# One adaLN gate and one layer's SSM preparation moved from VectorE to GpSimd

## The chip, the cores and the metric

The kernel runs on one NeuronCore of a Trainium2 chip. The metric is the device time of one execution in microseconds (us), the median of several runs. The engines are named as the profile names them: PE (TensorE matmul) and PEld (its weight load), DVE (VectorE), ACT (ScalarE), POOL (GpSimd) and SP (SyncE, which issues nearly all DMAs here). PEq, SPq and so on are the engines' instruction queues.

## The reference

Two layers of a hybrid decoder, sequence 256, model width 1024, all in float32:

```python
for l in range(2):
    mod = silu(c) @ w_ada[l] + b_ada[l]
    sh1, sc1, g1, sh2, sc2, g2 = split(mod, 6)            # 1024 each
    h = rmsnorm(x, norm1_g[l]) * (1 + sc1) + sh1
    u, dq, dk, dv, mq, mk, mv = split(h @ w_in[l])
    mix = concat(s5_mixer(u, ...), diff_attention(...), moba_attention(...))
    x = x + g1 * (mix @ w_out[l])
    h = rmsnorm(x, norm2_g[l]) * (1 + sc2) + sh2
    x = x + g2 * (relu(h @ mlp_w1[l])**2 @ mlp_w2[l])
return rmsnorm(x, final_g)
```

The S5 mixer is a complex diagonal state-space model. Before it can run in a layer it needs small weights made from the parameters (complex products of C and B with constants of the discretisation) and tables of sines and cosines for 128 steps of 8 pairs of groups.

## The kernel before

**Big products.** The weights come from HBM in units of 128 x 1024 floats (512 KB). `raw_unit` (L104) issues the DMA of a unit on SP into a ring `raw` of 3 buffers. `unit` (L112) splits it into a high part (ACT, L123) and a low part (DVE, L124) in a ring `whl` of 4 buffers, because each float32 product is made of three fp32r matmuls on PE (`mm3`, L129). A `raw` buffer comes free when both have read it, a `whl` buffer when PE has used it. The down projection of the MLP (`mlp2`, L983) uses two matmuls per tile of the hidden layer (L991, L992).

**adaLN vectors.** `mod` is 6 vectors of 1024 per layer, each a product of `silu(c)` with 8 units of `w_ada`. Those that are needed first are made by `ada_first`. The others go through `ada_two` (L283): it loads two units into the ring `ada` of 3 buffers and does one of two things. For most vectors PE multiplies them (`ada_mm`, L255). For the five in `ADA_DVE`, (layer 0, vector 2) and (layer 1, vectors 0 to 3), DVE accumulates them into one tile `adaacc`, scaled by a column of `cs` (L296, L298), and after the 8th unit four small matmuls sum over the partitions (L303). Vector (0, 2) is the gate g1 of the first mixer. Its units are asked for by the steps `D1` of the first layer's list of steps `MIXER[0]` (four pairs), those of layer 1 by the slots of the first layer's MLP (`ada_step_dve`, L1142). Steps `P` in the list ask for the units that PE multiplies, from the same ring `ada`. The gate is used in `back_add` after the output projection.

**SSM preparation.** `ssm_weights` (L595) gives three steps: two complex products of 128 x 256 tiles, with sign changes, for `cv`, and one for `ab` (22 elementwise instructions of 128 x 256 in all, lines 616 to 631). `ssm_tables` (L562) gives four steps `turns` (ACT instructions on L575 to L577, then three on engine `e`, L578 to L580) and one `sines` (ACT, and on `e` L588, twice). For layer 1 both are prepared in the first layer's MLP, one step per two slots from j = 1 on (L1143 to L1149), under `tc.issue_after` of the last DVE and ACT instruction. That call orders only instructions of the same engine as the one it names.

**Order.** Each engine runs its queue in order. SP's queue holds the DMAs of `raw`, `ada` and some others, and one whose buffer isn't free holds all those behind it. The order within the queues is not that of the text: a planner with costs of its own moves instructions, so that steps of the list interleave.

**POOL** builds a few constants at the start and adds up squares in the second half of each MLP (`square_in`, L1003, lines 1008 and 1010).

Of the kernel before, what the change touches and what calls it, by code (L numbers as in the profile page):

```python
# [14 lines left out]
OP = mybir.AluOpType  # L15
# [7 lines left out]
MAGIC = 12582912.0  # L23
# [31 lines left out]
def hybrid_trunk(ctx, tc, xT_d, pos_d, par_d, lqk_d, sb_d, sbt_d, scw_d, glu_d, wm_d, wa_d, out_d):  # L55
# [7 lines left out]
    V, A, T, GP = nc.vector, nc.scalar, nc.tensor, nc.gpsimd  # L63
# [4 lines left out]
    def wk_tile():  # L68
        return psum.tile([128, 512], F32, name="wk")
# [145 lines left out]
    cs = const.tile([128, 8], F32)  # L215
# [9 lines left out]
    def ada_finish(l, i, row):  # L225

        rs = work.tile([128, 256], F32, name="adarow", bufs=1)
        A.activation(rs, row, AF.Copy)

        def end():  # L230
            cp = wk_tile()
            for b in range(2):
                T.matmul(cp[:, 4 * b:4 * b + 4], rs[:, b * 128:(b + 1) * 128], ident[:, 0:128:32], start=True, stop=True)
            V.tensor_tensor(mod[l][:, i * 8:i * 8 + 8].rearrange("p (g b) -> p b g", b=2),
                            cp[:, 0:8].rearrange("p (b g) -> p b g", b=2),
                            col("b_ada", l * 48 + i * 8, 8).rearrange("p (g b) -> p b g", b=2), op=OP.add)
        return end
# [45 lines left out]
    def ada_two(l, i, k):  # L283

        ws = []
        for kk in (k, k + 1):
            w = ring.tile([128, UW], F32, name="ada", bufs=3)
            nc.sync.dma_start(w, wa_d[16 + ADA.index((l, i)) * 8 + kk])
            ws.append(w)
        if (l, i) in ADA_DVE:  # L290
            if k == 0:
                ada_st[l, i] = big.tile([128, UW], F32, name="adaacc", bufs=1)
            acc = ada_st[l, i]
            for j, w in enumerate(ws):
                if k + j == 0:
                    V.tensor_scalar(acc, w, cs[:, 0:1], None, op0=OP.mult)  # L296
                else:
                    V.scalar_tensor_tensor(acc, w, cs[:, k + j:k + j + 1], acc, op0=OP.mult, op1=OP.add)  # L298
            if k == 6:
                def fin():  # L300
                    row = wk_tile()[:, :256]
                    for g in range(4):
                        T.matmul(row[32 * g:32 * g + 32, :], ones, acc[:, g * 256:(g + 1) * 256], start=True, stop=True,  # L303
                                 tile_position=(0, 32 * g), skip_group_check=True)
                    return ada_finish(l, i, row)
                ada_fin_dve.append(fin)
        else:
            if k == 0:
                ada_st[l, i] = wk_tile()[:, :256]
            row = ada_st[l, i]  # L310
            for j in range(2):
                ada_mm(row, k + j, ws[j:j + 1])
            if k == 6:
                ada_fin.append(lambda: ada_finish(l, i, row))
# [247 lines left out]
    def ssm_tables(l, e):  # L562

        ct = big.tile([128, 8, 128], F32, name="tb_c")
        st = big.tile([128, 8, 128], F32, name="tb_s")
        TABS[l] = (ct, st)
        sh = [128, 2, 128]

        def turns(p):
            k = work.tile(sh, F32, name="sg_z")  # L570
            c = l * 8 + p
            a, r = ct[:, p:p + 2], st[:, p:p + 2]
            for j in range(2):
                i = slice(c + j, c + j + 1)
                A.activation(a[:, j], tau, AF.Copy, scale=f1[:, i])  # L575
                A.activation(r[:, j], tau, AF.Copy, scale=f2[:, i])
                A.activation(k[:, j], tau, AF.Identity, scale=f12[:, i], bias=magic)  # L577
            e.scalar_tensor_tensor(k, k, MAGIC, a, op0=OP.subtract, op1=OP.subtract)  # L578
            e.tensor_tensor(r, r, k, op=OP.subtract)
            e.tensor_scalar(r, r, -0.4999999, 0.4999999, op0=OP.max, op1=OP.min)  # L580

        def sines():
            for hp in range(0, NP, 4):
                r, c = st[:, hp:hp + 4], ct[:, hp:hp + 4]
                A.activation(c, r, AF.Sin, scale=math.pi)
                A.activation(r, r, AF.Sin, scale=2.0 * math.pi)
                A.activation(c, c, AF.Square)
                e.tensor_scalar(c, c, -2.0, 1.0, op0=OP.mult, op1=OP.add)  # L588
        return [lambda p=p: turns(p) for p in range(0, NP, 2)] + [sines]
# [340 lines left out]
    for l in range(L):  # L930
        V.tensor_scalar(subg[:, l:l + 1], col("subln", l), math.sqrt(128.0) * (1.0 - (0.8 - 0.6 * math.exp(-0.3 * l))), None,
                        op0=OP.mult)
# [66 lines left out]
    def x_rest():  # L999

        return (7,), sqsum[0], ones[:, 0:1], [work.tile([128, S], F32, name="sq", bufs=3)]
# [70 lines left out]
    for l in range(L):  # L1072
        mixed = [big.tile([128, 2, S], F32R, name=f"mx{k}") for k in range(KT)]

        if l == 0:
            h = hs
            cu, cm, cv_ = chunks
            uT = cu.u_out()
            v_m = cv_.values()
        else:  # L1080
            h = norm_h(l, "n1", 0, 1, x_rest(), vec)
            uT = Chunk("u", h).run().u_out()
            cm = Chunk("qk", h).run(1)
            v_m = None
        g2 = work.tile([128, 2, S], F32, name="g2", bufs=1)
        at, qk, accs = {}, {"m": cm}, []
        mix = {"m": slice(6, 8), "0": slice(2, 4), "1": slice(4, 6), "s": slice(0, 2)}
        for t in MIXER[l].split():
            o, a = t[0], t[1:]
            if o == "P":  # L1090
                ada_step(int(a), (l, 4))
            elif o == "D":
                ada_step_dve(int(a))
            elif o == "C":
                qk[a] = Chunk("qk", h).run()
            elif o == "R":
                at[a] = Attn(l, rope_T(qk[a]), v_m if a == "m" else None, a != "m", mixed[mix[a]])
            elif o == "S":
                ssm_two(l, int(a), uT)
            elif o == "E":  # L1100
                at[a[0]].scores(int(a[1]))
            elif o == "V":
                at[a].v = Chunk("v", h).run().values()
            elif o == "W":
                at[a[0]].values(int(a[1]))
            elif o == "F":
                at[a].finish()
            elif o == "Y":
                y = wk_tile()[:, :S]
                ssm_y(l, int(a), uT, y.rearrange("p (s b) -> p s b", s=2))  # L1110
                ssm_gelu(l, int(a), y, uT, g2)
            elif o == "O":
                ssm_out(l, g2, mixed[0:2])
            elif o == "K":
                if not accs:
                    accs = [acc_tile() for _ in range(4)]
                back_unit(accs, mixed[mix[a]], a == "m", False)
        while ada_fin or ada_fin_dve:
            flush(ada_fin)
            flush(ada_fin_dve)  # L1120
        vec = ada_load(l, 5)
        back_unit(accs, mixed[4:6], False, True)
        back_add(accs, l, 2)
        h = norm_h(l, "n2", 3, 4, x_ssq(), vec)
        slot = 0
        for half in range(2):
            acts = []
            for i in range(16):
                if i < 8:
                    acts += mlp1_act(mlp1_mm(h, 0 if half else i + 1), 2 * i)  # L1130
                else:
                    if half and l + 1 < L and i == 15:
                        vec = ada_load(1, 4)
                    mlp2(l, i - 8, acts)
                    if half and i < 15:
                        square_in(i - 8)
                j, odd = divmod(slot, 2)
                slot += 1
                if not odd:
                    continue  # L1140
                ada_step(1, (l, 5))
                ada_step_dve((0, 1, 1, 1, 2, 1, 2, 1, 2, 1, 1, 1, 1, 1, 0, 0)[j] if l == 0 else 0)  # L1142
                if l + 1 < L and j >= 1:  # L1143
                    if j == 1:
                        todo = list(ssm_weights(l + 1, V)) + ssm_tables(l + 1, V)
                        loads[l + 1]()
                    if todo:
                        with tc.issue_after(last_dve[0].ins), tc.issue_after(last_act[0].ins):
                            todo.pop(0)()  # L1149
                    elif j == 12:  # L1150
                        with tc.issue_after(last_mm[0].ins):
                            ssm_weights_pe(l + 1)
                        with tc.issue_after(last_act[0].ins):
                            rsqrt_table()
# [124 lines left out]
```

## Time and profile before

| | |
|---|---|
| median of 3 runs | 690.89 us (690.33 to 696.8) |
| the profiled execution | 694.18 us, span 692.5 us |
| PE busy in the span | 662.6 us (96%) |
| DVE busy | 508.6 us (73%) |
| ACT busy | 385.4 us (56%) |
| POOL busy | 19.2 us (3%), 23 instructions |
| granted TensorE clock | 0.997 of full |

Busy time is the time in which an engine works on an instruction. A row of the timeline gives start, duration, engine, line, operation, output and inputs, and in brackets how long the engine was idle before it and what ended that. Matmuls are pipelined, so the duration of one is longer than the distance to the next.

### The profile page before, as it was taken

To read this page: it belongs to the slowest core of one execution; us is meant where nothing else is said; L and a number is where in the kernel's file an instruction comes from. 1 tells how busy PE (TensorE), PEld (TensorE's weight loads), DVE (VectorE), ACT (ScalarE), POOL (GpSimd) and SP (SyncE) were. 2 spreads that over 40 slices of the span, in tenths; PEclk is the share of its full clock that TensorE was granted. 3 is DMA by queue.
4 is the path that set the end of the run, shared out by engine and by line. 5 is a ranking of instruction groups with operands and counts; after the bars stand their busy time and mean duration, and the time that the engine had idled before them with its cause. 6 is when DMAs were issued, how large, how long until landed. Compare 5 with 4: busy or idle time off the path is not lost. (4 is left out here: it accounts for less than half of the span.)

```text
span 692.5 us, 13248 instructions
## 1 busy us (share of the span) xinstructions
PE 662.6 (96%) x5134; PEld 576.0 (83%) x5134; DVE 508.6 (73%) x1148; ACT 385.4 (56%) x730; POOL 19.2 (3%) x23
## 2 busy tenths in 40 slices
PE   4998999999999999999999999999999999999994
PEld 1785777988899888998887878799899988999883
DVE  5869879976997887868657799876875655555653
ACT  4557555664566833677443547576476633566540
POOL 0000000000000000000220000000000000000220
PEclk9999999999999999999999999999999999999998
DMA  8986786863889698879855632554356555555531
GB/s 299 405 314 210 256 301 219 297 224 117 310 300 320 217 336 257 292 282 327 308 183 182 213 123 64 166 183 147 113 163 203 183 183 183 183 183 183 188 117 61
DMA packets 45278, 152.22 MB, mean 220 GB/s; under 512 B 5152, under 2 KB 5280, under 8 KB 45216
## 3 DMA queue, kind: packets, MB, share of 16 engines
q1 hardware_dynamic: 44640, 150.60, 63.1%
q10 hardware_dynamic: 576, 0.79, 0.4%
q8 instruction: 40, 0.66, 0.4%
q14 instruction: 22, 0.18, 0.1%
HBM read 150.32 MB, written 1.05 MB: 219 GB/s over the span
## 5 line engine op out<-in xcount | busy, mean ns | idle before, releaser
L124 DVE TENSOR_TENSOR whl<-raw,whl 128x1024 fp32r<-128x1024 f32 x178 | 217.4, 1224 | 109.5 <-ACT whl L123 106.7
L123 ACT ACTIVATE whl<-raw 128x1024 fp32r<-128x1024 f32 x178 | 187.8, 1056 | 149.9 <-DMA raw<-in_wm_dram 51.0
L132 PE MATMUL wk<-hx,whl 128*128 128x256 f32 x1536 | 188.5, 284 | 2.2 <-DVE hx L440 1.2
L132 PEld LDWEIGHTS wk<-hx,whl 128*128 128x128 f32 x1536 | 185.4, 192 | 5.5 <-DVE hx L440 2.5
L991 PE MATMUL acc<-mx,whl 128*128 128x512 f32 x256 | 92.1, 399 | 0.0
L992 PE MATMUL acc<-mx,whl 128*128 128x256 f32 x256 | 71.9, 281 | 0.0
L991 PEld LDWEIGHTS acc<-mx,whl 128*128 128x128 f32 x256 | 48.1, 188 | 12.1 <-issue 0.8
L298 DVE SCALAR_TENSOR_TENSOR adaacc<-ada,cs,adaacc 128x1024 f32<-128x1024 f32 x35 | 44.8, 1280 | 9.2 <-DMA ada<-in_wa_dram 9.1
L132 PE MATMUL acc<-mx,whl 128*128 128x256 f32 x384 | 51.1, 288 | 0.0
L132 PEld LDWEIGHTS acc<-mx,whl 128*128 128x128 f32 x384 | 47.4, 191 | 2.8 <-issue 2.7
L992 PEld LDWEIGHTS acc<-mx,whl 128*128 128x128 f32 x256 | 48.4, 189 | 0.3 <-DVE whl L124 0.3
L991 PE MATMUL acc<-at_e,whl 128*128 128x512 f32 x128 | 46.6, 398 | 0.0
L994 DVE SCALAR_TENSOR_TENSOR xall<-acc,mod,xall 128x256 f32<-128x256 f32 x64 | 30.9, 482 | 21.0 <-PE acc L992 20.2
L132 PE MATMUL acc<-whl,hx 128*128 128x256 f32 x288 | 40.0, 288 | 0.0
L132 PEld LDWEIGHTS acc<-whl,hx 128*128 128x128 f32 x288 | 36.5, 191 | 3.1 <-issue 2.2
L784 PE MATMUL acc<-whl,hx 128*128 128x512 f32 x96 | 38.7, 403 | 0.0
L783 PE MATMUL acc<-whl,hx 128*128 128x512 f32 x96 | 38.2, 401 | 0.0
L785 PE MATMUL acc<-whl,hx 128*128 128x512 f32 x96 | 38.0, 396 | 0.0
L992 PE MATMUL acc<-at_e,whl 128*128 128x256 f32 x128 | 35.9, 280 | 0.0
L972 ACT ACTIVATE sp_pa<-wk 128x512 f32<-128x512 f32 x32 | 18.9, 590 | 28.0 <-PE wk L132 28.0
L991 PEld LDWEIGHTS acc<-at_e,whl 128*128 128x128 f32 x128 | 24.0, 188 | 5.9
L439 ACT ACTIVATE hx<-hz,mod 128x256 fp32r<-128x256 f32 x32 | 14.9, 502 | 21.1 <-DVE hz L434 21.1
(352 smaller groups left out, 986.9 us busy)
## 6 DMA issues: line engine op xcount, KB each, us to landing
raw<-in_wm_dram SPq DMA_DIRECT2D x184, 512.0 KB, 4.0
ada<-in_wa_dram SPq DMA_DIRECT2D x74, 512.0 KB, 5.6
sp_gc<-in_wa_dram SPq DMA_DIRECT2D x9, 256.0 KB, 5.1
qT<-in_wa_dram SPq DMA_DIRECT2D x4, 512.0 KB, 8.7
adaacc<-in_wa_dram SPq DMA_DIRECT2D x3, 512.0 KB, 7.8
qk<-in_wa_dram SPq DMA_DIRECT2D x6, 256.0 KB, 5.4
vv<-in_wa_dram SPq DMA_DIRECT2D x6, 256.0 KB, 3.8
at_o<-in_wa_dram SPq DMA_DIRECT2D x6, 256.0 KB, 4.5
```

Of the source, the lines that this page charges most:

```text
L123: A.activation(hi, w, AF.Copy)
L124: V.tensor_tensor(lo, w, hi.bitcast(F32), op=OP.subtract)
L132: last_mm[0] = T.matmul(out, a[:, p, :], b[:, q, :], start=start and i == 0, stop=stop and i == 2, skip_group_check=True)
L298: V.scalar_tensor_tensor(acc, w, cs[:, k + j:k + j + 1], acc, op0=OP.mult, op1=OP.add)
L439: last_act[0] = A.activation(hi, z, AF.Identity, bias=mvec(l, i_sh, k))
L783: T.matmul(o, h[:, 0, sl], w[:, 0, :], start=(k == 0), stop=False, skip_group_check=True)
L784: T.matmul(o, h[:, 0, sl], w[:, 1, :], start=False, stop=False, skip_group_check=True)
L785: last_mm[0] = T.matmul(o, h[:, 1, sl], w[:, 0, :], start=False, stop=last, skip_group_check=True)
L972: A.activation(r, ps, AF.Relu)
L991: T.matmul(acc, w[:, 0, sl], a.rearrange("p c t -> p (c t)"), start=(k == 0), stop=False, skip_group_check=True)
L992: last_mm[0] = T.matmul(acc[:, :S], w[:, 1, sl], a[:, 0, :], start=False, stop=(k == 15), skip_group_check=True)
L994: V.scalar_tensor_tensor(xT[f], acc[:, c * S:(c + 1) * S], mvec(l, 5, f), xT[f], op0=OP.mult, op1=OP.add)
```

## The change

The accumulation of the units of layer 0's vector in `ada_two` is done on GpSimd, in two instructions per unit in place of one: it scales the unit in its `ada` buffer, and adds it to the accumulator. `ssm_weights` and `ssm_tables` of layer 1 get GpSimd as their engine. One instruction of `turns` stays on VectorE.

```diff
             for j, w in enumerate(ws):
-                if k + j == 0:
+                if l == 0:
+                    GP.tensor_scalar(acc if k + j == 0 else w, w, cs[:, k + j:k + j + 1], None, op0=OP.mult)
+                    if k + j:
+                        GP.tensor_tensor(acc, acc, w, op=OP.add)
+                elif k + j == 0:
                     V.tensor_scalar(acc, w, cs[:, 0:1], None, op0=OP.mult)
                 else:
                     V.scalar_tensor_tensor(acc, w, cs[:, k + j:k + j + 1], acc, op0=OP.mult, op1=OP.add)
...
-            e.scalar_tensor_tensor(k, k, MAGIC, a, op0=OP.subtract, op1=OP.subtract)
+            V.scalar_tensor_tensor(k, k, MAGIC, a, op0=OP.subtract, op1=OP.subtract)
             e.tensor_tensor(r, r, k, op=OP.subtract)
             e.tensor_scalar(r, r, -0.4999999, 0.4999999, op0=OP.max, op1=OP.min)
...
-                        todo = list(ssm_weights(l + 1, V)) + ssm_tables(l + 1, V)
+                        todo = list(ssm_weights(l + 1, GP)) + ssm_tables(l + 1, GP)
```

## Rows read from the trace of the kernel before

**Rows 1.** The page, busy time of each engine: us, share of the span, instructions.
```profile
PE 662.6 (96%) x5134; PEld 576.0 (83%) x5134; DVE 508.6 (73%) x1148; ACT 385.4 (56%) x730; POOL 19.2 (3%) x23
```

**Rows 2.** Stretches: length, busy PE, PEld, DVE, ACT, POOL, clock, DMA share, GB/s.
```profile
62.00:131.00 69.00, 66.48 (x530) 50.06 (x527) 61.27 (x185) 38.58 (x98) 0.00 (x0) 1.00 0.76 275
...
175.00:270.00 95.00, 93.57 (x651) 85.72 (x652) 81.51 (x127) 56.08 (x95) 0.00 (x0) 1.00 0.84 293
```

**Rows 3.** Waits of PE from 62 to 131 us: total us, times, longest.
```profile
PE wk L255 <- DMA ada<-in_wa_dram: 2.1, 3, 1.4
PE wk L821 <- ACT qT L822: 0.4, 1, 0.4
```

**Rows 4.** Tile adaacc from 55 to 170 us: count, ns min/median/max, first and last start.
```profile
L303 PE MATMUL wk<-adaacc,ones x8: 379/391/403, 155.2 to 156.7; 128*32 128x256 f32 x8
L298 DVE SCALAR_TENSOR_TENSOR adaacc<-ada,cs,adaacc x7: 1274/1281/1289, 71.1 to 128.1; 128x1024 f32<-128x1024 f32 x7
L296 DVE TENSOR_SCALAR adaacc<-ada,cs x1: 724/724/724, 67.9 to 67.9; 128x1024 f32<-128x1024 f32 x1
```

**Rows 5.** Timeline of POOL, both halves' accumulation of squares: start, duration.
```profile
331.82 1.19 POOL L1008 TENSOR_SCALAR sqs<-sq 128x256 f32<-128x256 f32 x1 [329.81 <-ACT sq L1005]
...
341.74 1.36 POOL L1010 TENSOR_TENSOR sqs<-sqs,sq 128x256 f32<-128x256 f32 x1 [5.08 <-ACT sq L1005]
...
661.45 1.30 POOL L1010 TENSOR_TENSOR sqs<-sqs,sq 128x256 f32<-128x256 f32 x1 [4.34 <-ACT sq L1005]
...
678.40 0.73 POOL L1010 TENSOR_TENSOR sqs<-sqs,sq 128x256 f32<-128x256 f32 x1 [4.36 <-ACT sq L1005]
```

**Rows 6.** Timeline of DVE beside the first two of these.
```profile
331.03 1.28 DVE L298 SCALAR_TENSOR_TENSOR adaacc<-ada,cs,adaacc 128x1024 f32<-128x1024 f32 x1
332.22 1.42 DVE L124 TENSOR_TENSOR whl<-raw,whl 128x1024 fp32r<-128x1024 f32 x1
...
341.28 1.23 DVE L124 TENSOR_TENSOR whl<-raw,whl 128x1024 fp32r<-128x1024 f32 x1
```

**Rows 7.** DVE groups by shape, whole span: count, busy us, mean ns.
```profile
L682 DVE TENSOR_TENSOR sp_pa<-sp_pa,sp_pb 128x256 f32<-128x256 f32 x8 | 3.4, 420 | 0.0
...
L580 DVE TENSOR_SCALAR tb_s<-tb_s 128x256 f32<-128x256 f32 x8 | 2.3, 286 | 0.0
```

**Rows 8.** Timeline of DVE: the second unit's accumulation, and a later split.
```profile
71.15 1.29 DVE L298 SCALAR_TENSOR_TENSOR adaacc<-ada,cs,adaacc 128x1024 f32<-128x1024 f32 x1 [1.91 <-DMA ada<-in_wa_dram]
...
78.83 1.20 DVE L124 TENSOR_TENSOR whl<-raw,whl 128x1024 fp32r<-128x1024 f32 x1
```

**Rows 9.** Timeline of SP's queue from 72 us.
```profile
72.46 0.33 SPq L288 DMA_DIRECT2D ada<-in_wa_dram  x1
72.83 0.43 SPq L109 DMA_DIRECT2D raw<-in_wm_dram  x1
```

**Rows 10.** Tile raw from 72 to 73 us: the one DMA, issue to landing.
```profile
DMA to landing us min/median/max: 5.3/5.3/5.3
```

**Rows 11.** Timeline of ACT: the split of the unit that this DMA brings.
```profile
78.27 1.06 ACT L123 ACTIVATE whl<-raw 128x1024 fp32r<-128x1024 f32 x1 [1.67 <-DMA raw<-in_wm_dram]
```

**Rows 12.** Timeline of PE's weight loads: the first use of that unit.
```profile
80.08 0.19 PEld L784 LDWEIGHTS acc<-whl,hx 128*128 128x128 f32 x1 [0.33 <-DVE whl L124]
```

**Rows 13.** Timeline of SP's queue, the raw DMA behind the second pair.
```profile
92.89 0.38 SPq L109 DMA_DIRECT2D raw<-in_wm_dram  x1
```

**Rows 14.** Timeline of ACT from 98 us.
```profile
98.69 1.04 ACT L123 ACTIVATE whl<-raw 128x1024 fp32r<-128x1024 f32 x1
```

**Rows 15.** Timeline of SP's queue: the last load for layer 1's SSM weights.
```profile
174.76 0.42 SPq L600 DMA_DIRECT2D sp_gc<-in_scw_dram  x1
```

**Rows 16.** Timeline of DVE: a split, and the first instruction of the SSM weights.
```profile
195.85 1.22 DVE L124 TENSOR_TENSOR whl<-raw,whl 128x1024 fp32r<-128x1024 f32 x1 [1.39 <-ACT whl L123]
...
204.38 0.42 DVE L616 TENSOR_TENSOR cv<-sp_gc,kre 128x256 f32<-128x256 f32 x1
```

**Rows 17.** Timeline of PE: the last eight units of the first up projection.
```profile
200.99 23.28 PE L132 MATMUL wk<-hx,whl 128*128 128x256 f32 x192
```

## The prediction

> **What bounds the kernel now.** I read the page first: PE is busy 96% of the span [rows 1], and POOL, which takes the moved work, is nearly empty. The reader is to see that PE can win at most what it idles, and where. The table of stretches gives that: from 62 to 131 us, where the gate's units are accumulated, PE is busy 66.5 of 69.0 us, and from 175 to 270 us, where layer 1's SSM weights and most of its tables are made, 93.6 of 95.0 us [rows 2]. So 2.5 and 1.4 us lie open in the places the change touches. DVE is full in both: 61.3 of 69.0 (89%) and 81.5 of 95.0 (86%). The waits of PE say whether that hurts: in the first stretch PE waits for DMAs of units that it multiplies itself and once for ACT, never for DVE [rows 3]. DVE is busy but ahead of PE, by little. Last I read the timelines for how little: which unit arrives just in time.
>
> **Prices on POOL.** An add of two 128x256 tiles takes 0.73 us when nothing is in its way; the others take about 1.3 us [rows 5]. The row at 341.74 ends at 343.10, and L124 on DVE, 341.28 to 342.51 [rows 6], ends 0.59 us before it: POOL waits for the split to end. Widths of 1024 are not in the trace on POOL. Bounds: no growth (0.7 us), and growth by four (2.9 us). DVE grows by 2.9 for an add (0.42 [rows 7] to 1.23 us [rows 6]) and by 2.5 for a scaling (0.29 [rows 7] to 0.72 us [rows 4]). With these factors the add costs 0.73 x 2.9 = 2.1 us. A scaling of width 256 ends 0.70 us after the L298 in its way (333.01 against 332.31 [rows 5, 6]), so one of 1024 costs 0.70 x 2.5 = 1.8 us. A unit thus takes 3.9 us on POOL where it took 1.28 us on DVE.
>
> **Removed.** DVE loses 7 x 1.28 + 0.72 = 9.7 us in the first stretch [rows 4]. In the MLP it loses 22 weight instructions (18 x 0.42 + 4 x 0.29 us) and ten of the tables (4 x 0.42, 4 x 0.29, and two of width 512 that I put at 0.42 us): 12.4 us. What PE can get back is bounded by its idle time, 2.5 + 1.4 us, and by 0, since it doesn't wait for DVE there; I take 0.
>
> **Added, the ring of loads.** A unit's `ada` buffer is free only when POOL has added it. The second unit lands at 71.15, where DVE stopped waiting for it, and DVE was through at 72.44 [rows 8]. At 72.46 SP issues the `ada` load that had waited for that buffer, and at 72.83, behind it in the queue, the DMA of a `raw` unit [rows 9], which lands 5.3 us later [rows 10]. ACT has stood idle 1.67 us for it [rows 11], L124 splits it from 78.83 to 80.03 [rows 8], and the weight load at 80.08 has waited 0.33 us for just this split [rows 12]. There is no slack in this chain. On POOL the unit is free at 71.15 + 3.9 = 75.05, 2.6 us later, and PE comes 2.6 us later to that product. Ends: 0.1 us (0.7 + 0.7 us on POOL) and 4.4 us (5.7 us on POOL). **I take 2.6.**
>
> The second pair holds the `raw` DMA at 92.89 [rows 13] in the same way. It could have landed at 98.2, ACT took it at 98.69 without a wait for the DMA [rows 14]; 2.6 us later makes it 2.1 us late for ACT. PE doesn't wait for a split here [rows 3], so I take 0 of 0 to 2.1. The last two pairs need 4 x 3.9 = 15.6 us on POOL. Even if it began only at 128.1, with DVE's last addition, it would end at 143.7, and the matmuls that sum over the partitions come at 155.2 [rows 4]: the gate itself costs nothing. Without those 11.5 us of cover PE would stand still at L303 with the output projection behind it.
>
> **Added, DVE against POOL.** One row shows DVE held by POOL: L124 at 332.22 took 1.42 instead of 1.23 us [rows 6] while POOL's scaling, waiting since 331.82, got its turn [rows 5]. So a POOL scaling of 256 costs the DVE instruction behind it 0.2 us. For an add, with twice the input, I use 0.4 us; its bounds are 0 and the 0.59 us. In the first stretch 15 POOL instructions at 0.2 x 2.5 = 0.5 us, or 1.0 for adds, make 8 x 0.5 + 7 x 1.0 = 11 us of delay against 9.7 us taken off DVE, which also idles 69.0 - 61.3 = 7.7 us: 0.
>
> In the MLP the POOL instructions are not held by the ordering calls, which bind DVE and ACT only. The last load they need is issued at 174.76 [rows 15], and by the 5.3 us of [rows 10] it has landed at about 180, while on DVE the work began at 204.38 [rows 16]. So it moves into the stretch in front, which is the fullest. The split of 195.85 to 197.07 [rows 16] is, by count, the unit in front of the eight that PE begins at 200.99 (192 matmuls in 23.28 us, 0.121 us each [rows 17]); PE needs it at about 200.99 - 24 x 0.121 - 0.4 (four small matmuls) = 197.7. It has 0.6 us of slack, and DVE idled 1.39 us in front of it: 2.0 us of cover. From 180 to 195.85 POOL gets in some ten instructions, one for each of DVE's of 1.2 us. At 0.2 us each that is 2.0, covered; at 0.4 us 4.0, so 2.0 late; at 0.59 us 3.9 late. **I take 1.0**, between the first two.
>
> The tables add a way from DVE over POOL to ACT: the last two `turns` write a buffer that POOL must have read, 0.3 to 0.9 us later each than now, and the splits of ACT queue behind. I cost it at 0 under the four `whl` buffers; without that cover it is up to 1.8 us.
>
> **The sum.** The profiled execution took 694.18 us; + 2.6 + 1.0 gives 697.8. It stands 3.3 us above the median of the runs, 690.89, so the median becomes 694.5 us.
>
> **A rule against the change.** By the row at 332.22 DVE lost 0.2 us to a POOL instruction of 0.7 us [rows 5, 6]. The Trainium skill, "SBUF — State Buffer", section "Who interferes with whom", says that the two share a port pair with an exclusive lock: a VectorE instruction with two SBUF inputs and a GpSimd one that reads SBUF block each other fully, for the whole instruction. POOL's waits agree, DVE's 0.2 us doesn't, and by that rule the time would be that of the next case.
>
> **Rival: DVE is held for POOL's whole instructions, and becomes the bound.** 8 x 1.8 + 7 x 2.1 = 29.1 us of POOL in the first stretch, against 17.4 us that DVE then has free: 0 to 11.7 us too much, as its instructions that read PSUM are hit or spared; I take 5. In the MLP 3.9. With the 2.6 us of the ring: 690.89 + 11.5 = 702.4 us, from 698 to 711. It decides once an add of 1024 holds DVE for more than about 1.5 us. Against it stands the one row.
>
> **Rival: nothing comes late.** The planner may put the `raw` DMA in front of the `ada` load, or start the pairs earlier, since it orders by costs and POOL's differ; or POOL's instructions hardly grow with width. Then the change does its work unseen: 688.4 (2.5 us of idle time returned) to 691.5 us. For it: queues are visibly not in the order of the text. Against it: the chain at 72 to 80 us is tight by 0.0 us.
>
> **Rival: DVE's relief counts.** All 3.9 us of idle time return: 687.0 us. More would need another order of PE's own work, which the profile doesn't offer.
>
> **Chances.** A measurement of this kernel can tell about 1%, 6.9 us, from no change. Forecast (691.5 to 697.8) 0.52, nothing late 0.25, the lock 0.20, relief 0.03. Slower than 697.8: all but 0.01 of the lock and 0.03 of the forecast's upper end, 0.22. Faster than 684.0: 0.03, with a new order of the queues. The same: 0.75. The range of 688 to 702 us leaves out the upper half of the lock and most of the relief.
>
> **What would show it.** A later `raw` DMA than 72.83 and a longer wait of PE for L124 near 80 us show the ring; POOL rows of 1.8 and 2.1 us the prices; L124 or L298 longer than 1.3 us, or gaps beside POOL rows, the lock; the first L616 on POOL near 181 us and a wait for L124 near 198 us the MLP's term. I am wrong if PE waits in none of these places, or if the gate's last sum on POOL comes after 155 us and PE stops at L303.

## The result and the profile after

The changed kernel takes **712.8 us** (median of 6 runs, 709.82 to 717.87) against 690.69 us of the kernel before beside it: 1.0325 times as long, 95% interval 1.029 to 1.0359. The forecast was 694.5 us, the range 688 to 702 us. It was wrong, and beyond the rival that would have made it slower too (702.4 us).

The profiled execution took 710.61 us, its span is 709.0 us. On its page, busy time by engine [rows 1 for before]:

```profile
PE 665.9 (94%) x5134; PEld 578.6 (82%) x5134; DVE 517.0 (73%) x1108; ACT 385.1 (54%) x730; POOL 100.6 (14%) x70
```

The work moved (POOL 19.2 to 100.6 us), yet DVE is busy 8.4 us longer with 40 instructions fewer. The stretches [rows 2], with one between them that I had not looked at:

```profile
62.00:131.00 69.00, 60.96 (x447) 43.68 (x447) 58.54 (x167) 31.75 (x86) 29.25 (x11) 0.93 0.65 227
131.00:175.00 44.00, 37.86 (x334) 35.03 (x334) 30.92 (x71) 23.74 (x58) 12.99 (x5) 0.96 0.58 196
175.00:270.00 95.00, 89.98 (x699) 80.95 (x698) 78.92 (x100) 55.39 (x101) 37.45 (x30) 1.00 0.74 255
```

PE gets through 447 matmuls in the first stretch where it got through 530, and the clock is no longer 1.00. By the first matmul of the up projection PE is 14.9 us late (189.70 against 174.82 us). The profiled executions lie 16.4 us apart, so nearly all of it is lost in the first mixer. POOL there, the first pair and the last five units [rows 5 is all that before showed of POOL]:

```profile
64.43 3.34 POOL L296 TENSOR_SCALAR adaacc<-ada,cs 128x1024 f32<-128x1024 f32 x1 [62.41 <-DVE whl L124]
67.76 3.00 POOL L296 TENSOR_SCALAR ada<-ada,cs 128x1024 f32<-128x1024 f32 x1
70.84 2.38 POOL L298 TENSOR_TENSOR adaacc<-adaacc,ada 128x1024 f32<-128x1024 f32 x1
...
124.14 2.35 POOL L298 TENSOR_TENSOR adaacc<-adaacc,ada 128x1024 f32<-128x1024 f32 x1
126.47 3.28 POOL L296 TENSOR_SCALAR ada<-ada,cs 128x1024 f32<-128x1024 f32 x1
129.84 2.39 POOL L298 TENSOR_TENSOR adaacc<-adaacc,ada 128x1024 f32<-128x1024 f32 x1
132.19 2.86 POOL L296 TENSOR_SCALAR ada<-ada,cs 128x1024 f32<-128x1024 f32 x1
135.13 2.49 POOL L298 TENSOR_TENSOR adaacc<-adaacc,ada 128x1024 f32<-128x1024 f32 x1
137.60 4.08 POOL L296 TENSOR_SCALAR ada<-ada,cs 128x1024 f32<-128x1024 f32 x1
141.75 2.41 POOL L298 TENSOR_TENSOR adaacc<-adaacc,ada 128x1024 f32<-128x1024 f32 x1
```

A unit behind the first takes POOL 5.3 to 6.6 us, not 3.9. Now SP's queue from 121 us. Each DMA goes out as soon as an addition above has ended (126.49, 132.23, 137.62, 144.16 us):

```profile
121.17 0.38 SPq L109 DMA_DIRECT2D raw<-in_wm_dram  x1
126.52 0.33 SPq L288 DMA_DIRECT2D ada<-in_wa_dram  x1
132.25 5.73 SPq L264 DMA_DIRECT2D ada<-in_wa_dram  x2
138.03 0.42 SPq L273 DMA_DIRECT2D qk<-in_wa_dram  x1
144.19 0.33 SPq L264 DMA_DIRECT2D ada<-in_wa_dram  x1
144.62 0.37 SPq L273 DMA_DIRECT2D qk<-in_wa_dram  x1
145.08 0.86 SPq L109 DMA_DIRECT2D raw<-in_wm_dram  x2
```

For 24 us no `raw` DMA is issued. L264 loads the next vector into the same ring `ada`. The `raw` DMAs behind it are the weights of the output projection. What follows is read in the timelines of ACT, DVE and PE:

```profile
150.73 1.06 ACT L123 ACTIVATE whl<-raw 128x1024 fp32r<-128x1024 f32 x1 [6.48 <-DMA raw<-in_wm_dram]
```
```profile
151.82 1.22 DVE L124 TENSOR_TENSOR whl<-raw,whl 128x1024 fp32r<-128x1024 f32 x1 [4.18 <-ACT whl L123]
152.97 0.16 DVE L147 SCALAR_TENSOR_TENSOR at_rq<-rs_t,rs_i 128x4 f32<-128x4 f32 x1
153.16 0.76 DVE L920 TENSOR_TENSOR at_on<-at_o,at_rq 128x256 f32<-128x256 f32 x2
```
```profile
153.73 0.68 PE L925 MATMUL wk<-ident,at_on 128*128 128x128 f32 x4 [1.92 <-DVE at_on L920]
```

ACT waits 6.48 us for the unit, DVE 4.18 us for ACT. The last step of a chain of small instructions (L147), which does not need the unit, stands behind that split in DVE's queue, and PE waits 1.92 us for what L920 makes of its result.

A second effect is on DVE's timeline. Three rows begin while an addition is at work (the additions end at 73.22, 98.45 and 103.99 us). The two small ones end with it, at 98.48 and 104.02 us; the split ends at 74.30 us, 1.1 us behind it, nearly its usual time of 1.22 us:

```profile
71.44 2.86 DVE L124 TENSOR_TENSOR whl<-raw,whl 128x1024 fp32r<-128x1024 f32 x1
...
96.43 2.05 DVE L861 TENSOR_SCALAR at_m<-at_m 128x4 f32<-128x4 f32 x1
...
102.22 1.80 DVE L913 TENSOR_TENSOR at_ms<-at_q,at_r 128x8 f32<-128x8 f32 x1
```

L913 takes 0.15 us at 145.16 us, on half the width, where no addition is beside it. A third effect is in PE's clock, the third column from the right, in steps of 2 us:

```profile
112.00:114.00 2.00, 0.80 (x6) 0.59 (x6) 2.00 (x6) 0.47 (x1) 0.00 (x0) 1.00 0.80 240
114.00:116.00 2.00, 0.62 (x4) 0.40 (x4) 2.00 (x13) 0.59 (x1) 0.00 (x0) 1.00 0.81 258
116.00:118.00 2.00, 2.00 (x24) 1.79 (x23) 2.00 (x6) 0.95 (x2) 0.00 (x0) 0.95 0.89 334
118.00:120.00 2.00, 0.94 (x7) 0.46 (x10) 1.97 (x6) 0.00 (x0) 0.00 (x0) 0.50 1.00 387
```

PE idles 2.6 of 4 us, and then runs at 0.50, the lower of its two levels (1.2 GHz). So three causes stood there at once: loads held in SP's queue, DVE held by POOL, and the clock. The trace shows each, but not what each costs.

### The profile page after: what moved, and what is told of

It reads as the page before. It is cut to its first block, busy times and chain, and to the rows that moved or that the text cites. A ratio compares the mean times of both kernels' runs of the same rounds, so it can differ in the third digit from the quotient of the medians.

```text
span 709.0 us, 13285 instructions
## 1 busy us (share of the span) xinstructions
PE 665.9 (94%) x5134; PEld 578.6 (82%) x5134; DVE 517.0 (73%) x1108; ACT 385.1 (54%) x730; POOL 100.6 (14%) x70
## 5 line engine op out<-in xcount | busy, mean ns | idle before, releaser
L124 DVE TENSOR_TENSOR whl<-raw,whl 128x1024 fp32r<-128x1024 f32 x178 | 224.8, 1266 | 118.5 <-ACT whl L123 115.6
L1012 POOL TENSOR_SCALAR sqs<-sq 128x256 f32<-128x256 f32 x2 | 3.1, 1541 | 315.7 <-ACT sq L1009 315.7
L132 PE MATMUL acc<-whl,hx 128*128 128x256 f32 x288 | 41.9, 296 | 0.0
L132 PEld LDWEIGHTS acc<-whl,hx 128*128 128x128 f32 x288 | 38.5, 200 | 3.0 <-issue 2.0
L302 DVE SCALAR_TENSOR_TENSOR adaacc<-ada,cs,adaacc 128x1024 f32<-128x1024 f32 x28 | 37.6, 1343 | 2.2 <-DMA ada<-in_wa_dram 2.1
L866 ACT ACTIVATE at_e<-at_e,at_m 128x128 f32<-128x128 f32 (+1 forms) x48 | 21.2, 443 | 17.8 <-DVE at_m L861 17.7
```

Source lines behind the costliest of these rows:

```text
L124: V.tensor_tensor(lo, w, hi.bitcast(F32), op=OP.subtract)
L132: last_mm[0] = T.matmul(out, a[:, p, :], b[:, q, :], start=start and i == 0, stop=stop and i == 2, skip_group_check=True)
L866: A.activation(e[:, c, ks], e[:, c, ks], AF.Exp, scale=SCALE, bias=mx[:, i:i + 1], accum_out=st[:, i:i + 1])
```

## The experiments

**First: which part, and is it the order?** The planner had written another order of all queues. Four kernels: the gate alone on POOL (e1), the SSM preparation alone (e2), the work of before in the order of e1 (f1), and e1's work in the order of before (f2).

```diff
 e1: -  list(ssm_weights(l + 1, GP)) + ssm_tables(l + 1, GP)
     +  list(ssm_weights(l + 1, V)) + ssm_tables(l + 1, V)
 e2: -  if l == 0:        # in ada_two
     +  if False:
 f1, f2: each queue tied to the other kernel's order, by dependences without a semaphore
```

> The gate's units on POOL, the SSM preparation back on DVE. In the trace after the change the first mixer ends 14.9 us later than before (183.5 against 168.6 us) and the first up projection adds 4.5 us more. If the gate makes the first and the SSM preparation the second, this kernel is 13 to 16 us above the one before (704 to 707 us). If the loss in the mixer came from the planner's reaction to both moves, it is within 7 us of the one before.

> The SSM preparation on POOL, the gate's units on DVE. If the two moves cost apart, 1 to 5 us above the one before (692 to 696 us): POOL's adds of 256 columns hold DVE for 0.6 us each while the up projection starts. If the SSM part is harmless by itself and was only late because the mixer was, 0 +- 1 us. More than 7 us would say that most of the loss is here.

> The kernel before (gate and SSM preparation on DVE), with the instructions of PE, ACT, SP and DVE put in the order that the planner wrote for e1 (the eight gate instructions of DVE where the planner wants them). Theory POOL (its instructions hold DVE, and its buffers hold the loads): within 3 us of the one before. Theory order (the planner, with POOL's costs, wrote a worse order): 8 to 15 us above it, as slow as e1.

> e1 with the instructions of PE, ACT, SP and DVE put in the order of the kernel before. Theory POOL: 8 to 16 us above the one before, about e1 or worse, since nothing in the order makes room for units that stay on POOL for 5.3 us. Theory order: within 4 us of the one before.

Measured: e1 1.0265 (1.0222 to 1.0309), e2 1.0056 (1.0033 to 1.0079), f1 1.0088 (1.0054 to 1.0122), f2 1.0181 (1.0117 to 1.0245). The gate is four fifths of the loss (2.65 of 3.25%). The order seems to be the smaller part of that: with the work of before it costs 0.9%, and the gate on POOL in the order of before costs 1.8%. The intervals of f2 and e1 overlap a little, so this split is rough.

**Second: held buffers or held DVE?** Four variants of e1; g1 to g3 leave the sum over the units out, so they are for timing alone. In g1 the additions become scalings; in g2 POOL frees each buffer with a tiny read and then adds the accumulator to itself; g3 has only the tiny reads; in g4 each addition comes in four quarters. PE, DVE, ACT and SP keep the order of e1, so the same weight load can be found in each trace by counting.

```diff
 g1: -  GP.tensor_tensor(acc, acc, w, op=OP.add)
     +  GP.tensor_scalar(acc, w, cs[:, 0:1], None, op0=OP.mult)
 g2: +  GP.memset(acc, 0.5)                                          # once
     +  GP.tensor_scalar(acc[:, k + j:k + j + 1], w[:, 0:1], ...)    # per unit
     +  GP.tensor_tensor(acc, acc, acc, op=OP.add)                   # per unit, behind both reads
 g3: as g2, without the tensor_tensor
 g4: -  GP.tensor_tensor(acc, acc, w, op=OP.add)
     +  for c in range(0, UW, 256):
     +      GP.tensor_tensor(acc[:, c:c + 256], acc[:, c:c + 256], w[:, c:c + 256], op=OP.add)
```

> The gate alone on POOL as in e1, in the same order of all queues, but each addition of a unit to the accumulator is replaced by a second scaling of that unit into the accumulator (one input in place of two); the sum over the units is left out. The unit's ada buffer is held as long as in e1 or longer (two scalings of about 2.9 us). Lock theory (the additions hold DVE for their whole length of 2.4 us, the scalings hardly): DVE's rows beside POOL are of normal length, and most of e1's 18.7 us goes: 694 to 700 us. Ring theory (the loss comes from SP's queue, held by loads whose buffer POOL has not released): as e1, 706 to 713 us. If both matter about alike: 700 to 705 us.

> The same order of all queues as e1, but POOL frees each pair of ada buffers with two reads of 128 x 1, and then makes the additions of 128 x 1024 on the accumulator alone (accumulator plus accumulator); the units are left out of the sum. So POOL's additions stay, 7 of 2.4 us, and no load waits for POOL. Lock theory: the additions alone cost most of it, 702 to 709 us. Ring theory: 694 to 698 us, at the level of the kernel before in this order (696.4 us).

> As the run with POOL's additions on the accumulator alone, but without these additions: POOL only reads 128 x 1 of each unit, and the accumulation is left out. Neither lock nor ring. Both theories: 692 to 697 us, at or under the 696.4 us of the kernel before in this order, since DVE has its 9.7 us of accumulation less. If it stays above 700 us, the loss is neither of the two but sits in the order of the queues.

> e1 in the same order of the other engines' queues, each addition of 128 x 1024 on POOL made as four of 128 x 256 (about 0.7 us each). Lock theory: a DVE instruction that reads two tiles of SBUF now waits for a quarter, no longer for 2.4 us, but each quarter meets another DVE instruction; POOL waits for DVE in turn: 700 to 706 us, with DVE rows lengthened by at most about 0.8 us. Ring theory: the unit's buffer is free later than in e1, 707 to 714 us.

| | POOL works on a buffer | additions | ratio | 95% interval |
|---|---|---|---|---|
| g3 | 0.3 to 0.7 us | none | 1.0012 | 0.9979 to 1.0044 |
| g2 | 0.3 to 0.5 us; one pair 4.3 us, behind additions | 7 of about 2 us | 1.0066 | 1.0037 to 1.0094 |
| e1 | 5.3 to 6.3 us | 7 of 2.4 us | 1.0265 | 1.0222 to 1.0309 |
| g1 | 5.7 to 6.9 us | none | 1.0298 | 1.0268 to 1.0327 |
| g4 | 5.7 to 7.8 us | 28 of about 0.7 us | 1.0319 | 1.0288 to 1.0351 |

My theory after reading the trace was the lock, POOL's additions holding DVE; as the main cause it falls. The lock is real: the split L124, as grouped rows of DVE from 90 to 145 us, e1 first and then g1:

```profile
L124 DVE TENSOR_TENSOR whl<-raw,whl 128x1024 fp32r<-128x1024 f32 x7 | 12.8, 1835 | 1.3 <-ACT whl L123 1.3
```
```profile
L124 DVE TENSOR_TENSOR whl<-raw,whl 128x1024 fp32r<-128x1024 f32 x7 | 9.0, 1283 | 0.0
```

Without additions the mean falls from 1835 to 1283 ns, and the kernel is no faster; POOL's work on a buffer is about 0.5 us longer there. The additions alone cost 1.0066 - 1.0012 = 0.5%, about 4 us, the one pair of g2 that waited behind them included. With the buffers free at once the loss is gone. What holds SP's queue in e1 (total us, times, longest):

```profile
SPq L288 <- POOL adaacc L298: 20.1, 4, 5.7
SPq L264 <- POOL adaacc L298: 15.5, 3, 5.3
...
SPq L288 <- POOL adaacc L296: 3.1, 1, 3.1
```

In g3 POOL holds it 3.4 us in all. How late PE is, by the same weight load (first transposes of the second `at_on`, L935 or L925), g3, e1 and g1:

```profile
137.83 0.42 PEld L935 LDWEIGHTS wk<-ident,at_on 128*128 128x128 f32 x4 [0.20 <-issue]
```
```profile
155.02 0.71 PEld L925 LDWEIGHTS wk<-ident,at_on 128*128 128x128 f32 x4 [3.60 <-issue]
```
```profile
158.62 0.72 PEld L925 LDWEIGHTS wk<-ident,at_on 128*128 128x128 f32 x4 [6.12 <-issue]
```

Counting weight loads also shows where e1 loses its time. Two loads of units for PE's own vectors, L262 in g3 and L255 in e1:

```profile
91.28 0.16 PEld L262 LDWEIGHTS wk<-ada,crep 128*32 128x32 f32 x8 [0.33 <-issue]
...
115.94 0.16 PEld L262 LDWEIGHTS wk<-ada,crep 128*32 128x32 f32 x8 [1.68 <-DMA ada<-in_wa_dram]
```
```profile
93.31 0.16 PEld L255 LDWEIGHTS wk<-ada,crep 128*32 128x32 f32 x8 [0.33 <-issue]
...
120.41 0.20 PEld L255 LDWEIGHTS wk<-ada,crep 128*32 128x32 f32 x8 [1.44 <-DMA ada<-in_wa_dram]
```

In front of the first pair (56.06 us in g3, 55.16 us in e1) e1 was 0.9 us ahead. It is 2.0 us behind at the first of these loads and 4.5 us at the second, just before POOL begins the third pair (122.70 us). At `at_on` it is 17.2 us behind. So in these two traces the first two pairs cost e1 5.4 us, and the stretch of the last two 12.7 us.

**Third: what is it that the held buffers delay?** h1 holds a buffer for one scaling only (about 3 us, no addition, no sum). h2 is e1, but on SP three `raw` DMAs move ahead of the loads L264 and L273. h3 also moves `raw` DMAs ahead of loads that wait for POOL in the first two pairs. h4 is h3 with the scalings of g1.

```diff
 h1: -  GP.tensor_scalar(acc if k + j == 0 else w, w, cs[:, k + j:k + j + 1], None, op0=OP.mult)
     -  if k + j:
     -      GP.tensor_tensor(acc, acc, w, op=OP.add)
     +  GP.tensor_scalar(acc, w, cs[:, k + j:k + j + 1], None, op0=OP.mult)
 h2, order of SP:
     -  ada(L288) ada(L264) x2 qk ada(L264) qk raw raw sp_gc raw
     +  ada(L288) raw raw raw ada(L264) x2 qk ada(L264) qk sp_gc
```

> e1 in the same order of PE, DVE, ACT and SP, but POOL only scales each unit into the accumulator, once; the sum over the units is left out. The unit's buffer is held 2.9 us in place of 5.3 and POOL makes no addition. Hold theory (time grows with how long POOL holds an ada buffer; so far 1.001 at 0.3 us, 1.0265 at 5.3, 1.030 at 5.7): in between, 696 to 704 us. If a threshold decides (second unit of a pair landing while the first is in work): near 692 to 696. Lock theory has nothing to add here, as no addition is made.

> e1 complete, with the same order on PE, DVE, ACT and POOL; on SP alone the six loads of the next vector (L264, L273) that stood in front of three raw DMAs behind the last pair of the gate come after these. Theory that the raw DMAs behind the held loads cost the time: the raw DMAs that e1 issued at 146.5 us go out as soon as their buffers are free, from about 137 us, PE's waits at 150 to 155 us go, 5 to 8 us of e1's 18 come back: 700 to 705 us. Rival, the additions' lock on DVE sets the time in that stretch: the split that frees a raw buffer is late by itself, and little comes back, 706 to 710 us.

> As the run with the late loads moved, and also the loads that wait for POOL in the first and second pair stand behind one or two raw DMAs more. Theory of the raw DMAs: all of the hold but its effect on PE's own units goes, 695 to 700 us, near the run with the additions and a free ring (696.0 us). Rival, the late loads of units that PE multiplies cost as much: 702 to 710 us.

> As the run with the raw DMAs ahead in all places, but each addition replaced by a second scaling (the sum over the units is left out), so that DVE isn't held by additions while the buffers are held for as long. The difference to that run is the lock: by the run with additions and a free ring against that without, 0.5%, 3 to 4 us, so 692 to 697 us if the raw DMAs were the hold's whole cost. If it stays above 703 us, the hold costs through PE's own units and the order on SP doesn't matter.

Measured: h1 1.0100 (1.0027 to 1.0174), h2 1.0173 (1.0147 to 1.0199), h3 1.0186 (1.0154 to 1.0218), h4 1.011 (1.0073 to 1.0148). h1 lies between g3 and e1, as its hold does, though its interval is wide. 1.0265 - 1.0173 = 0.9% (6 us) is the three `raw` DMAs behind the late loads alone. They now go out at 138.60 us, and PE comes to the weight load above 4.9 us earlier than in e1:

```profile
138.60 4.81 SPq L116 DMA_DIRECT2D raw<-in_wm_dram  x3
```
```profile
150.15 0.48 PEld L932 LDWEIGHTS wk<-ident,at_on 128*128 128x128 f32 x4 [1.50 <-issue]
```

Moving the earlier `raw` DMAs as well won nothing (h3). It is not that PE waits longer for late `ada` loads: from 62 to 160 us it waits 1.3 us for them in h3 and 3.6 us in h2. What h3 loses instead stands in the fourth step. With `raw` DMAs ahead, the additions cost 1.0186 - 1.011 = 0.8%.

**Fourth: is the rest the clock, and where do the SSM instructions hurt?** In h4 PE's clock is 0.50 from 119 to 131 us, and PE is busy nearly throughout. What that costs can be counted, since PE's order is the same in g3, h4 and the other variants in e1's order. From the first load of L262 below to the next transposes of `at_e` (L902, in h4 L899) PE loads the same 71 weights, in g3 and in h4:

```profile
115.94 0.16 PEld L262 LDWEIGHTS wk<-ada,crep 128*32 128x32 f32 x8 [1.68 <-DMA ada<-in_wa_dram]
...
125.35 0.35 PEld L902 LDWEIGHTS wk<-ident,at_e 128*128 128x128 f32 x3
```
```profile
119.59 0.20 PEld L262 LDWEIGHTS wk<-ada,crep 128*32 128x32 f32 x8 [2.64 <-DMA ada<-in_wa_dram]
...
134.28 0.35 PEld L899 LDWEIGHTS wk<-ident,at_e 128*128 128x128 f32 x3
```

That is 9.41 us in g3 and 14.69 us in h4. PE has no gap in either; the clock is 1.00 in g3 and 0.58 on average in h4:

```profile
116.00:125.50 9.50, 9.49 (x72) 7.54 (x73) 7.04 (x34) 5.09 (x19) 1.31 (x4) 1.00 0.92 316
```
```profile
119.60:134.50 14.90, 14.90 (x73) 11.67 (x74) 7.01 (x31) 5.30 (x19) 13.37 (x5) 0.58 0.33 115
```

So the lower clock costs h4 5.3 us here, about half of the 10.5 us that it is behind g3 at `at_on` (148.33 against 137.83 us). In h1, at 1.00, the same loads take 9.41 us again. In e1 they take 10.82 us, in h2 10.68 (clock 0.87), in f1 12.78 (0.74), in h3 15.24 (0.64) and in the changed kernel 13.77 (0.69); PE idles 0.6, 1.2 and 0.9 us of the last three. So this stretch takes 4.6 us more in h3 than in h2, which may be what the moved DMAs could have won. The 3.4 us of f1 are as much as its profiled span exceeds that of g3 (692.4 against 689.0 us).

k1 (on h2), k2 (on f1) and k3 (on h4) put 12 extra matmuls, which wait for nothing, on PE in front of the first transposes of `at_on`, where it idled. s1 is e2 with the SSM loads and steps four slots later.

```diff
 k1 to k3: +  for q in range(12):
           +      T.matmul(tp[32 * (q % 4):32 * (q % 4) + 32, 0, :], crep[:, 0, :], crep, start=True, stop=True, ...)
 s1: -  if l + 1 < L and j >= 1:
     -      if j == 1:
     +  if l + 1 < L and j >= 3:
     +      if j == 3:
```

> The run with the raw DMAs ahead of the late loads (h2, complete), and on PE 12 extra matmuls (128 x 32 by 128 x 256, with no wait, result not used) right in front of the first transposes of at_on, where PE stood idle 3.0 us in that run before its clock was granted at 0.50 from about 117 to 125 us. They take about 2.3 us that PE would idle. Clock theory (part of the loss is not the waits but the lower clock that follows an idle PE): the granted clock from 62 to 131 us rises from 0.93 to 0.98 or more, and 3 to 5 us come back: 698 to 701 us. Rival, the clock has nothing to do with this idle time, or the loss is only the waits: 703 to 706 us.

> The work of before (gate on DVE) in the order of e1's queues (f1, 696.4 us, ratio 1.009), with the same 12 extra matmuls on PE. In f1 PE idled about 2.4 us at 114 to 118 us, and the clock was granted at about 0.5 for two stretches up to 128 us (0.95 over the stretch from 62 to 131 us), with no POOL work at all. Clock theory: clock 0.99 or more, ratio 1.001 to 1.005. Rival, DVE's work in this order is late in itself: ratio 1.008 to 1.012.

> The run without additions and with the raw DMAs ahead (h4, 699.3 us, ratio 1.011), and the same 12 extra matmuls in the same place on PE. In h4 PE idled 1.4 us there and 2.6 us five microseconds later, and its clock was granted at 0.50 from 119 to 132 us while PE was busy without a gap, which by the positions of the same loads of weights made it 5 us later. Nothing but PE seems to bind in this stretch. Clock theory, kept for this case: the clock stays at 1.00 there and the ratio falls to 1.003 to 1.007. Rival, supported by the run with additions where the clock came back and no time did: DVE, ACT and the DMAs set the pace there as well, ratio 1.008 to 1.014.

> The SSM weights and tables alone on POOL (e2, ratio 1.0056), but their loads and steps begin four slots later in the MLP. In e2 POOL's instructions lay at 178 to 205 us, beside the hx tiles that PE waits for, 4.0 us in place of 1.2. Place theory (my forecast's MLP term: POOL moves into the fullest stretch and holds DVE there): begun after the hx tiles, the wait for hx falls to about 1.2 us and the ratio to 0.998 to 1.003. Rival, POOL's instructions hold DVE's splits wherever they lie: 1.004 to 1.008.

Measured: k1 1.0186 (1.0146 to 1.0226), k2 1.0087 (1.0054 to 1.012), k3 1.0072 (1.0037 to 1.0107). In k1 the clock came back and the time did not change measurably; the stretch from 62 to 131 us, h2 and k1:

```profile
62.00:131.00 69.00, 62.52 (x461) 44.75 (x462) 55.64 (x165) 31.40 (x84) 24.96 (x10) 0.93 0.64 220
```
```profile
62.00:131.00 69.00, 61.10 (x481) 42.79 (x480) 56.40 (x164) 32.57 (x83) 23.43 (x9) 0.98 0.66 229
```

By the count there was little to win: the 71 loads take 9.43 us in k1 (clock 1.00) and 10.68 in h2, and 1.3 us is less than the two intervals can tell. In k2 and k3 the clock fell all the same (0.90 and 0.91 over this stretch), after other idle spots, so their times don't test it. Of the 12 timed runs of k3 the five with a mean clock up to 0.986 took 698.2 to 700.8 us, the seven from 0.989 on 691.4 to 696.6 us. That agrees with a price of the clock, but these runs were not made to differ in it; the count above is the stronger evidence.

s1 gives 1.0022 (0.9987 to 1.0057), e2 1.0056; the intervals overlap, so the times don't tell the two apart. The traces are plainer: PE's wait for `hx` is 1.2 us in the kernel before, 4.0 in e2, 3.4 after the change and 1.4 in s1. DVE's pairs of L444 that PE waits for, e2 and s1:

```profile
180.50 1.58 DVE L444 SCALAR_TENSOR_TENSOR hx<-hz,mod,hx 128x256 fp32r<-128x256 f32 x2
...
185.20 1.70 DVE L444 SCALAR_TENSOR_TENSOR hx<-hz,mod,hx 128x256 fp32r<-128x256 f32 x2
```
```profile
179.91 0.88 DVE L444 SCALAR_TENSOR_TENSOR hx<-hz,mod,hx 128x256 fp32r<-128x256 f32 x2
...
182.69 0.88 DVE L444 SCALAR_TENSOR_TENSOR hx<-hz,mod,hx 128x256 fp32r<-128x256 f32 x2
```

In s1 POOL begins at 181.79 us, with the last pair, where in e2 it began at 178.13 us.

No version beat the kernel before. With the gate's accumulation left out altogether (g3) the time is that of before. g3 has e1's order, though, and within that order taking the work off DVE won 0.8% (f1 to g3). What it would win in the order of before no run shows.

## Why the prediction was wrong

- **What bounds the kernel.** That PE's idle time, 2.5 + 1.4 us [rows 2], was all there was to win agrees with g3, which wins nothing measurable (0.9979 to 1.0044, in e1's order). I looked at the two stretches in which POOL's instructions lie, not at the one behind them, and 131 to 175 us lost 5.8 us of busy PE (43.65 us before, 37.86 after).
- **Prices on POOL.** I took 2.1 us for an addition and 1.8 us for a scaling from rows of a quarter of the width [rows 5, 6]. They measure 2.43 and 3.14 us on average, 2.35 and 2.84 at least. The addition was near. The scaling, with one input, costs more than the addition with two, which no ratio of DVE gives: 2.84 us is four times my 0.70 us of a quarter of the width, where DVE's ratio was 2.5. The upper bound I kept, 5.7 us a unit, was near the truth.
- **The ring, the step that failed.** The mechanism was right and I priced it once, in the first pair (2.6 us). There it came true: ACT's split at 79.06 us had waited 5.99 us for its `raw` unit, where it had waited 1.67 [rows 11], and e1 loses 2.9 us there. The second pair, which I took at 0 of 0 to 2.1 us, costs another 2.5 us by 120 us. For the last two pairs I asked only when the sum of the accumulator is needed (155.2 us [rows 4]) and wrote that "the gate itself costs nothing". That looks at what POOL produces. What POOL holds has other users: three loads of L264 wait for these buffers, and the `raw` DMAs stand behind them in SP's queue. In the trace of before these L264 rows follow at 119.79 and 129.45 us, one `raw` DMA behind the last of them at 131.42; I did not go down SP's queue that far. Measured, the three `raw` DMAs there cost 0.9% by themselves (h2), and the stretch of the last two pairs costs e1 12.7 us in its trace. All that the held buffers cost, with the big scalings and the idle PE's lower clock that come with them, is 1.0265 - 1.0066 = 2.0%, 14 us, where I had 2.6.
- **The lock.** I priced it by one row, 0.2 us, scaled it to 0.4 us and 1.0 us for additions, and let DVE's idle time cover it. The rows after show DVE held to the addition's end, up to 2.1 us beyond its own time (L124 at 141.90 takes 3.34 us), and g1 shows it held little by scalings. For additions the Trainium skill, "SBUF — State Buffer", section "Who interferes with whom", had it right: a VectorE instruction with two SBUF inputs and a GpSimd one that reads SBUF lock each other out for the whole instruction. The trace agrees with it for additions, and the rival I built on it was right in its mechanism for these. It does not agree for scalings, which read SBUF too: in g1 an L124 that begins at 141.60 us, in the middle of a scaling (139.77 to 142.62 us), takes 1.22 us. The rival's price of 5 us in the mixer is near the measured 0.5 to 0.8%, 4 to 5 us. It missed the total because the ring was the larger part. (Its range of 698 to 711 us begins, by its own terms, at 697.4, and reaches 711 only with the ring's upper end of 4.4 us.)
- **The MLP.** Right place and mechanism, as far as the traces of e2 and s1 show, too small and in another row: it was not a split near 198 us but the `hx` pairs, 3.4 us of waits in place of 1.2. The SSM preparation costs 0.6% (4 us) where I had 1.0 us. In the changed kernel POOL began at 194.47, not 181 us, because the mixer in front was late.
- **Not foreseen.** The clock, which was 1.00 in every stretch I had read: where PE has idled, the work behind runs at 0.50 for some us, 13.77 us for 71 weight loads in the changed kernel against 9.41 in g3. And the planner's new order, from which I had expected help at best ("nothing comes late"). With the gate on DVE it costs 0.9% (f1; in its trace 3.4 us of that in the stretch of the lower clock), and nothing with no gate work in it (g3).
- **Open.** h4 is 1.1% above the kernel before. Its trace gives 5.3 us to the lower clock and 3.8 us to loads that PE itself waits for, but no run takes either away alone: k1 filled one idle spot, and in k2 and k3 the clock fell elsewhere. Whether the idle time in front of the low clock comes from POOL's hold in each kernel is not shown; f1 has it with no gate work on POOL.

## What to carry to other kernels

Before work moves to a slower engine, list the buffers that it reads, and for each the DMA that waits for it and everything behind that DMA in the same queue: the price is paid there, even where the result itself has time to spare. When a trace shows a lock, a held queue and a fallen clock together, kernels that remove one at a time tell their sizes, and where the order of the queues is the same, counting the same instructions in two traces tells where the time went. Here the loudest rows (DVE held 2 us at a time) were a fifth to a third of the gate's loss. A cover proves nothing about the stretch after it: read on until the waits of all queues are as before.

## What the hardware showed that I had not expected

- On POOL the shortest scaling of 128 x 1024 by a column takes 2.84 us, the shortest addition of the same size 2.35 us, and a scaling of 128 x 1 0.28 us (g3).
- An addition on POOL holds even a DVE instruction on 128 x 4 with one input (L861, 2.05 us where the one at 103.94 us takes 0.16). Scalings beside L124 lengthen it little (g1, 1283 ns on average; 1225 is the median in the kernel before), and it is the scaling that grows: the one at 145.64 us in g1, beside an L124 of 1.23 us, takes 3.90 us.
- Cutting the addition into quarters (g4) doesn't help: four take 2.8 to 4.9 us, and the buffer is held longer.
- PE's granted clock fell to 0.50 after PE had idled 2.6 of 4 us, and in k1, with idle spots of 1.07 and 1.94 us about five microseconds apart, it stayed at 1.00.
